# Seven products in place of eight for w2's column chunks, and splits placed two plain blocks ahead, in a float32 decoder layer

## The chip, the core and the metric

The kernel runs on one core of a Trainium2 chip. The core has five engines that run beside each other, each with its own queue in program order, and meet through semaphores: TensorE (PE; PEld is its loading of stationary tiles), VectorE (DVE), ScalarE (ACT), GpSimd (POOL) and SyncE (SP), which here issues most DMAs. The metric is the device time of one execution in microseconds: 2285.92 us before, the median of three runs (2285.74 to 2286.81).

## The reference

One decoder layer on 256 positions of width 2048, in float32: two SwiGLU blocks with a mixer of four branches between them, each behind an RMSNorm and added to the residual x. The change touches the SwiGLUs alone:

```
h = h + 0.5 * swiglu(rms_norm(h, ffn1_norm[l]), ffn1_w1[l], ffn1_w3[l], ffn1_w2[l])
h = h + hybrid_mixer(rms_norm(h, mix_norm[l]), w_in[l], conv_w[l], ...)
h = h + 0.5 * swiglu(rms_norm(h, ffn2_norm[l]), ffn2_w1[l], ffn2_w3[l], ffn2_w2[l])

def swiglu(x, w1, w3, w2):
    return (jax.nn.silu(x @ w1) * (x @ w3)) @ w2
```

w1 and w3 are 2048 x 5632, w2 is 5632 x 2048.

## The kernel before

**Float32 from three products.** The kernel feeds TensorE rounded operands (the type F32R). Each is split into a high part (a cast by ScalarE to the rounded type) and a low part (VectorE: the value minus the high part), and a product a*b is three matmuls: low by high, high by low, high by high. A *step* below is one such matmul of a 128x128 stationary tile with 512 columns.

**Blocks.** The weights stream through in blocks of 256 rows by 512 columns (KB = 2 times 128 rows), 512 KB each. `load` (L254) brings one into a `raw` buffer (six of them), `split` (L268) makes `whi` and `wlo` from it (three buffers each, LA + 1), `multiply` (L292) runs its matmuls. A *plain* block is 2 (rows of 128) x 2 (halves of the 256 positions) x 3 = 12 steps.

**Groups and pairs.** `Group` (L207) is one column chunk: 8 blocks for 2048 rows, two PSUM accumulators. `Pair` (L132) works two chunks with the same stationary side at once, here chunk c of w1 and chunk c of w3: 16 blocks, alternating between the two matrices, four accumulators `acc`. A *quad* is two row blocks by two column chunks, that is two blocks of the list. Six of a pair's eight quads are plain (12 + 12 steps). Quads 0 and 3 (SQ, L27) use a Strassen-like scheme of seven products (`seven`, L162) in place of eight: 21 steps in place of 24. So blocks 0 and 6 of a pair carry no product, and blocks 1 and 7 carry a seven each. For a seven `prepare` (L221) makes sums and differences of the two weight blocks in five steps (step 0: L233 to L235, 1: L237 to L239, 2: L241 to L243, 3: L245 and L246, 4: L248), and `combine` (L384) those of the normalised input, once per SwiGLU and quad; four of the seven products go to `common` (four `wk` banks of PSUM), which `join` (L181) adds up one and two blocks behind the second seven.

**A SwiGLU** (L462) has three parts of 4, 4 and 3 column chunks of h. In each, w1's and w3's chunks come first (chunk 0 as two Groups, the others as Pairs); at the end of a pair `done` and `gated` (L202, L470) add the shares and form h, and `fill` (L413) transposes it through TensorE some blocks later into `hhi` and `hlo`. Then w2 multiplies the part's h into x: four Groups of 8 blocks (6 in part 2), one for each 512 columns of x, and `add` (L484) adds half of each to x from PSUM.

**What sets the order.** Everything is issued by one loop over the blocks (L849). At block i it issues the loads that are due, the split of block i + 2 (LA), the due step of `prepare` (step 5 - j for a seven whose left block is j blocks ahead, LEAD = 5: steps 0 to 4 at five blocks in a row), then block i's matmuls, then the work posted for i (`later`: joins, transposes, combine). Each engine runs its own part strictly in that order; a wait is set where data or a buffer is not there.

Of the kernel before, what the change touches and what calls it, by code (L numbers as in the profile page):

```python
# [14 lines left out]
P = 128  # L15
# [11 lines left out]
SQ = (0, 3)  # L27
LEAD = 5
EPS = 1e-6
# [10 lines left out]
def hybrid_mixer_kernel(  # L40
# [91 lines left out]
    class Pair:  # L132

        n, nk = NQ, NK

        def __init__(self, w1, w3, col0, norm, gated):
            self.norm, self.gated, self.ps = norm, gated, None  # L140
            self.common, self.i0 = None, len(blocks)
            for q in range(NK // KB):
                for w in (w1, w3):
                    ap = w[q * KB * P:(q + 1) * KB * P, col0:col0 + NQ]
                    if q in SQ:
                        early_blocks[len(blocks)] = w is w1
                    blocks.append([self, q * KB, ap.rearrange("(k p) n -> p k n", p=P), None, None])
# [14 lines left out]
        def seven(self, k0, ops7):  # L162
            self.open()
            b11, b21, b22, t1, t2, t3, t4 = ops7
            q = k0 // KB
            s1, s2, s3, s4 = self.norm.sums[q]
            first, last = q == SQ[0], q == SQ[-1]
            a = {(t, k): self.norm.stat(k0 + k, t) for t in range(NT) for k in range(KB)}
# [12 lines left out]
        def join(self, step):  # L181

            c = self.common
            if step == 0:
                c0, u, v, w = (tmp() for _ in range(4))
                self.share = {(0, 0): c0, (0, 1): u, (1, 0): v, (1, 1): w}
                nc.scalar.copy(c0, c[0])
                nc.vector.tensor_add(u, c[1], c0)
                nc.vector.tensor_add(v, c[2], u)
            else:  # L190
                u, v, w = (self.share[i] for i in ((0, 1), (1, 0), (1, 1)))
                nc.vector.tensor_add(u, c[3], u)
                nc.vector.tensor_add(w, c[3], v)

        def plain(self, k0, j, hi, lo):
            for k in range(KB):
                for t in range(NT):
                    last = k0 + k == NK - 1
                    self.product(self.ps[t, j], self.norm.stat(k0 + k, t), (hi[k], lo[k]),
                                 (t, j) == (1, 1) and k0 + k == 2 and 0 in SQ, last)  # L200

        def done(self, _):  # L202
            for i in ((0, 0), (1, 0), (0, 1), (1, 1)):
                nc.vector.tensor_add(self.share[i], self.ps[i], self.share[i])  # L204
            self.gated(self.share)

# [107 lines left out]
    def later(d, f, *a):  # L314
        posts.setdefault(now[0] + d, []).append((f, a))
# [23 lines left out]
    class Norm:  # L339
        def __init__(self, i):  # L340
            self.i = i
            self.ss = sb.tile([P, NT, 4], F32, name=f"ss{i}")
            self.r = sb.tile([P, NT], F32, name=f"rstd{i}")
            self.hi, self.lo = {}, {}
            self.both, self.sums = {}, {}

        def squares(self, c, tiles=range(NT)):
            for t in tiles:
                junk = sb.tile([P, NQ], F32, name="junk")
                nc.scalar.activation(junk, xr[t, c], AF.Square, accum_out=self.ss[:, t, c:c + 1])  # L350
# [32 lines left out]

        def combine(self, q):  # L384

            if not self.sums:
                self.s_hi = ops.tile([P, 2, 4, P], F32R, name="sph", bufs=1)
                self.s_lo = ops.tile([P, 2, 4, P], F32R, name="spl", bufs=1)
            hi, lo = self.both[q]
            v, s = tmp().rearrange("p (k s) -> p k s", k=KB), tmp().rearrange("p (i s) -> p i s", i=4)  # L390
            nc.vector.tensor_add(v, hi.bitcast(F32), lo.bitcast(F32))
# [4 lines left out]
            nc.vector.tensor_sub(s[:, 3], a12, s[:, 1])  # L396
            n = len(self.sums)
            split_to(self.s_hi[:, n], self.s_lo[:, n], s)
            self.sums[q] = [(self.s_hi[:, n, i], self.s_lo[:, n, i]) for i in range(4)]

    class Parts:
# [11 lines left out]
        def fill(self, c, src):  # L413

            hi, lo = self.chunk(c)
            for j in range(2):
# [5 lines left out]
                split_to(hi[:, 2 * j:2 * j + 2], lo[:, 2 * j:2 * j + 2], tp)  # L422

        def stat(self, base):
            def f(k, t):
# [10 lines left out]

    def first_pair(norm, w1, w3, h):

        for j, q in enumerate(SQ):
            posts.setdefault(len(blocks) + 10 + 3 * j, []).append((norm.combine, (q,)))  # L440
        act = {}
# [19 lines left out]

    def swiglu(norm, w1, w3, w2, finish):  # L462
        for part, (c0, c1) in enumerate(((0, 4), (4, 8), (8, 11))):
            h = Parts()
            for c in range(c0, c1):
                if c == 0:
                    first_pair(norm, w1[0], w3[0], h)
                    continue

                def gated(p, i=c - c0, h=h, n=3 if c + 1 == c1 else FILL):  # L470
                    hs = [tmp() for _ in range(NT)]
# [9 lines left out]

                Pair(w1[0], w3[0], c * NQ, norm, gated)
            for c in range(4):
                def add(p, tiles=range(NT), c=c, part=part):  # L484
# [3 lines left out]
                    if part == 2:  # L488
                        finish(c, tiles)

# [16 lines left out]
    def mixer(norm, finish):  # L507
# [239 lines left out]
        qc = to_heads(QC, r8)  # L747
        kc = sb.tile([P, 2, S], F32, name="kc")
        vc = sb.tile([P, NT, P], F32, name="vc")
# [89 lines left out]
    for i in range(LA):  # L839
        norms[0].transposed(0, (i,))  # L840
        split(i)

    turn = sorted(range(5, len(blocks)),
                  key=lambda i: i - 0.5 - LEAD // 2 - (not early_blocks[i]) if i in early_blocks else i)
    at_turn = {}
    for i in turn:
        k = max(0, (i - (not early_blocks[i]) - LEAD - 2) if i in early_blocks else i - 5)
        at_turn.setdefault(k, []).append(i)
# [62 lines left out]
```

## Time and profile before

| | before |
|---|---|
| median of three runs | 2285.92 us |
| the profiled execution | 2286.18 us |
| its span, first to last instruction | 2284.3 us |
| TensorE / VectorE / ScalarE busy | 2257.2 / 1507.4 / 1101.0 us |
| granted TensorE clock, mean | 0.998 |
| matmuls | 10250 |

Matmuls of 512 columns overlap: each is on record for about 0.39 us, but the next starts earlier. So TensorE's pace is read from starts, and a wait shows in brackets behind a row: the idle time before it and who ended it.

### The profile page before, as it was taken

To read this page: it belongs to the slowest core of one execution; us is meant where nothing else is said; L and a number is where in the kernel's file an instruction comes from. 1 tells how busy PE (TensorE), PEld (TensorE's weight loads), DVE (VectorE), ACT (ScalarE), POOL (GpSimd) and SP (SyncE) were. 2 spreads that over 40 slices of the span, in tenths; PEclk is the share of its full clock that TensorE was granted. 3 is DMA by queue.
4 is the path that set the end of the run, shared out by engine and by line. 5 is a ranking of instruction groups with operands and counts; after the bars stand their busy time and mean duration, and the time that the engine had idled before them with its cause. 6 is when DMAs were issued, how large, how long until landed. Compare 5 with 4: busy or idle time off the path is not lost.

```text
span 2284.3 us, 26894 instructions
## 1 busy us (share of the span) xinstructions
PE 2257.2 (99%) x10250; PEld 1854.3 (81%) x10250; DVE 1507.4 (66%) x1765; ACT 1101.0 (48%) x1316; POOL 6.7 (0%) x22
## 2 busy tenths in 40 slices
PE   8999999999999999999999999999999999999998
PEld 6888888888888887778888888888888888888886
DVE  5885587756875566664565555556875678757875
ACT  5554444444545445454565444455544445444543
POOL 0000000000000000000000000000000000000000
PEclk9999999999999999999999999999999999999999
DMA  6565666656655655556655666556665665566564
GB/s 223 185 209 182 194 197 195 192 187 200 187 193 184 192 175 160 170 166 187 182 166 174 193 193 188 185 177 182 203 199 186 195 203 184 184 198 199 184 215 135
DMA packets 222776, 428.56 MB, mean 188 GB/s; under 512 B 13436, under 2 KB 15544, under 8 KB 222648
## 3 DMA queue, kind: packets, MB, share of 16 engines
q1 hardware_dynamic: 222128, 425.78, 59.9%
q8 instruction: 80, 1.31, 0.2%
q10 hardware_dynamic: 520, 1.08, 0.1%
q14 instruction: 48, 0.39, 0.0%
HBM read 424.71 MB, written 2.10 MB: 187 GB/s over the span
## 4 chain that ended last, share of the span: by engine, by line
PE 87%; DVE 8%; ACT 2%; issue 2%; DMA 0%; SPq 0%; POOL 0%; DVEq 0%; POOLq 0%; ACTq 0%
PE acc L307 18%; PE acc L308 18%; PE acc L309 18%; PE acc L159 9%; PE acc L160 9%; PE acc L158 8%; DVE wlo L289 3%; ACT whi L288 1%; DVE tmp L204 1%; PE wk L159 1%; PE wk L160 1%; PE wk L158 1%; PE wk L421 1%; DVE tq L248 1%; DVE at L237 1%
## 5 line engine op out<-in xcount | busy, mean ns | idle before, releaser
L289 DVE TENSOR_TENSOR wlo<-raw,whi 128x1024 fp32r<-128x1024 f32 (+1 forms) x725 | 874.1, 1215 | 643.9 <-ACT whi L288 639.7
L288 ACT CAST whi<-raw 128x1024 fp32r<-128x1024 f32 (+1 forms) x725 | 752.7, 1046 | 821.5 <-PE acc L309 497.0
L307 PE MATMUL acc<-whi,xlo 128*128 128x512 f32 (+1 forms) x992 | 389.0, 392 | 5.5 <-DVE xlo L335 3.7
L308 PE MATMUL acc<-wlo,xhi 128*128 128x512 f32 (+1 forms) x992 | 384.8, 388 | 3.3 <-DVE wlo L289 3.3
L309 PE MATMUL acc<-whi,xhi 128*128 128x512 f32 (+1 forms) x992 | 383.7, 387 | 0.0
L159 PE MATMUL acc<-wlo,xhi 128*128 128x512 f32 x960 | 375.3, 391 | 3.7 <-DVE wlo L289 3.7
L158 PE MATMUL acc<-whi,xlo 128*128 128x512 f32 x960 | 375.0, 391 | 0.0
L160 PE MATMUL acc<-whi,xhi 128*128 128x512 f32 x960 | 373.9, 389 | 0.0
L307 PE MATMUL acc<-whi,hlo 128*128 128x512 f32 x912 | 357.0, 391 | 2.3 <-DVE tmp L204 2.3
L309 PE MATMUL acc<-whi,hhi 128*128 128x512 f32 x912 | 355.2, 389 | 0.0
L308 PE MATMUL acc<-wlo,hhi 128*128 128x512 f32 x912 | 355.2, 389 | 0.0
L307 PEld LDWEIGHTS acc<-whi,xlo 128*128 128x128 f32 x992 | 186.6, 188 | 47.8 <-ACT whi L288 4.6
L308 PEld LDWEIGHTS acc<-wlo,xhi 128*128 128x128 f32 x992 | 186.8, 188 | 41.8 <-DVE wlo L289 5.9
L309 PEld LDWEIGHTS acc<-whi,xhi 128*128 128x128 f32 x992 | 186.8, 188 | 38.1
L159 PEld LDWEIGHTS acc<-wlo,xhi 128*128 128x128 f32 x960 | 180.2, 188 | 45.6 <-DVE wlo L289 9.1
L158 PEld LDWEIGHTS acc<-whi,xlo 128*128 128x128 f32 x960 | 180.3, 188 | 37.1
L160 PEld LDWEIGHTS acc<-whi,xhi 128*128 128x128 f32 x960 | 180.2, 188 | 37.0
L307 PEld LDWEIGHTS acc<-whi,hlo 128*128 128x128 f32 x912 | 171.2, 188 | 39.9 <-issue 5.0
L309 PEld LDWEIGHTS acc<-whi,hhi 128*128 128x128 f32 x912 | 171.2, 188 | 35.9
L308 PEld LDWEIGHTS acc<-wlo,hhi 128*128 128x128 f32 x912 | 171.3, 188 | 35.2 <-DVE wlo L289 0.4
L332 DVE TENSOR_TENSOR hlo<-wk,hhi 128x512 fp32r<-128x512 f32 (+1 forms) x64 | 38.6, 637 | 49.2 <-ACT hhi L331 49.2
L245 ACT CAST tq<-raw 128x1024 fp32r<-128x1024 f32 x40 | 42.2, 1055 | 49.6 <-DVE raw L243 49.6
(205 smaller groups left out, 1739.3 us busy)
## 6 DMA issues: line engine op xcount, KB each, us to landing
raw<-in_ffn_w_dram SPq DMA_DIRECT2D x527, 512.0 KB, 4.1
raw<-in_w_in_dram SPq DMA_DIRECT2D x208, 512.0 KB, 3.6
raw<-in_w_branch_dram SPq DMA_DIRECT2D x32, 512.0 KB, 3.6
raw<-in_w_out_dram SPq DMA_DIRECT2D x32, 512.0 KB, 3.9
x<-in_x_dram SPq DMA_DIRECT2D x8, 256.0 KB, 6.4
raw<-in_w_in_dram SPq DMA_DIRECT2D x8, 256.0 KB, 2.8
out_dram<-x SPq DMA_DIRECT2D x8, 256.0 KB, 2.6
tq<-in_final_norm_dram ACTq DMA_DIRECT2D x2, 512.0 KB, 4.3
```

Source lines behind the costliest of these rows:

```text
L158: nc.tensor.matmul(o, sl, wh, start=start, stop=False)
L159: nc.tensor.matmul(o, sh, wl, start=False, stop=False)
L160: nc.tensor.matmul(o, sh, wh, start=False, stop=stop)
L204: nc.vector.tensor_add(self.share[i], self.ps[i], self.share[i])
L237: nc.vector.tensor_sub(d["bl"], raw1, d["bh"].bitcast(F32))
L245: nc.scalar.copy(d["th1"], raw1)
L288: nc.scalar.copy(h, r)
L289: nc.vector.tensor_sub(l, r, h.bitcast(F32))
L307: nc.tensor.matmul(o, sl, wh, start=(k == 0), stop=False)
L308: nc.tensor.matmul(o, sh, wl, start=False, stop=False)
L309: nc.tensor.matmul(o, sh, wh, start=False, stop=(k == g.nk - 1))
L332: nc.vector.tensor_sub(lo, src, hi.bitcast(F32))
```

## The change

w2 of parts 0 and 1 of each SwiGLU is worked in Pairs too: two pairs of column chunks (0 with 1, 2 with 3) in place of four Groups, each with the two sevens. Part 2 (six row blocks) stays with Groups. `Pair` takes its two matrices, the stationary side, the sums and what to do at the end as arguments. The sums get a class of their own; there is one buffer for them, so they are made for the norm, then for the part's h in the last w1 and w3 pair of the part (blocks 10 and 12), and for the norm again in the second w2 pair (blocks 9 and 11). A w2 pair adds its joined shares to x in the middle (`joined`, in three join steps) and its four accumulators at the end (`rest`).

The loop's plan is new as well. Splits count plain blocks: at a plain block the split of the plain block two further on in the list is issued, so blocks 2 and 3 of a pair are split at blocks 14 and 15 of the one before. Loads come three blocks ahead of the split. The five steps of `prepare` begin 7 blocks ahead of quad 0 and 5 ahead of quad 3, steps 0 and 1 at one block and the rest at the next three: for block 0 at blocks 9 to 12 of the pair before, formerly 11 to 15. The last chunk of h is transposed 10 blocks behind its pair in parts 0 and 1, formerly 3.

```
-LEAD = 5
+LEAD = {0: 7, 3: 5}
 ...
+    class Sums:
+        def make(self, q, both):
+            n = SQ.index(q)
+            if n == 0:
+                self.hi = ops.tile([P, 2, 4, P], F32R, name="sph", bufs=1)
+                self.lo = ops.tile([P, 2, 4, P], F32R, name="spl", bufs=1)
+            hi, lo = both()
+            v = sb.tile([P, KB, S], F32, name="kc", bufs=1)
+            s = sb.tile([P, 4, P], F32, name="junk", bufs=1)
             nc.vector.tensor_add(v, hi.bitcast(F32), lo.bitcast(F32))
 ...
+            split_to(self.hi[:, n], self.lo[:, n], s)
 ...
+        def make_at(self, i, both):
+            for j, q in enumerate(SQ):
+                posts.setdefault(i + 2 * j, []).append((self.make, (q, lambda q=q: both(q))))
 ...
             if last:
-                later(1, self.join, 0)
-                later(2, self.join, 1)
+                for step in range(3 if self.joined else 2):
+                    later(1 + step, self.join, step)
 ...
+                if c + 1 == c1 and part < 2:
+                    h_sums.make_at(len(blocks) + 10, h.both)
+                Pair([w[0][:, c * NQ:(c + 1) * NQ] for w in (w1, w3)], norm.stat, sums, gated)
+            for c in range(0, 4, 2) if part < 2 else ():
+                def joined(i, share, c=c):
+                    y = xr[i[0], c + i[1]]
+                    nc.vector.scalar_tensor_tensor(y, share, 0.5, y, op0=OP.mult, op1=OP.add)
+
+                def rest(p, joined=joined):
+                    for i in ((0, 0), (1, 0), (0, 1), (1, 1)):
+                        joined(i, p[i])
+
+                if c == 2:
+                    sums.make_at(len(blocks) + 9, norm.both.get)
+                Pair([w2[0][c0 * NQ:c1 * NQ, j * NQ:(j + 1) * NQ] for j in (c, c + 1)], h.stat(0),
+                     h_sums, rest, joined)
 ...
+    plain = [i for i in range(len(blocks)) if i not in early_blocks]
+    splits, loads, steps = {}, {}, {}
+    for p in range(LA, len(plain)):
+        n = plain[p - LA]
+        splits[n] = plain[p]
+        if plain[p] >= 5:
+            loads.setdefault(max(0, n - 3), []).append((n, plain[p]))
+    for i, left in early_blocks.items():
+        if left:
+            n = i - LEAD[(blocks[i][1] // KB)]
+            loads.setdefault(n - 2, []).extend([(n, i), (n, i + 1)])
+            for j in range(5):
+                steps.setdefault(n + max(0, j - 1), []).append((i, j))
 ...
-        for j in at_turn.get(i, ()):
+        for _, j in sorted(loads.get(i, ())):
             load(j)
-        split(i + LA)
-        for j in range(1, LEAD + 1):
-            if early_blocks.get(i + j):
-                prepare(i + j, LEAD - j)
+        if i in splits:
+            split(splits[i])
+        for j in steps.get(i, ()):
+            prepare(*j)
```

How this moves VectorE's instructions is seen at two places. The first is the end of an ordinary pair of w1 and w3. Before, the last steps of the next seven's preparation (L246, L248), the closing work (L204, L475, L478), and only then the splits of the next pair's blocks 2 and 3 (L289 x2):

```order
L246 TENSOR_TENSOR tq<-raw,tq 128x1024
L248 TENSOR_TENSOR tq<-raw,tq 128x1024
L204 TENSOR_TENSOR tmp<-acc,tmp 128x512 x4
L475 SCALAR_TENSOR_TENSOR tmp<-tmp,rstd_95 128x512 x2
L478 SCALAR_TENSOR_TENSOR tmp<-tmp,rstd_95 128x512 x2
L289 TENSOR_TENSOR wlo<-raw,whi 128x1024 x2
L235 TENSOR_TENSOR raw<-raw 128x512
L289 TENSOR_TENSOR wlo<-raw,whi 128x1024
```

Now, at the same place (L300 is the split, L215, L501 and L504 the closing work, L246 to L250 steps 0 and 1 of `prepare` for block 7's seven):

```order
L259 TENSOR_TENSOR tq<-raw,tq 128x1024
L300 TENSOR_TENSOR wlo<-raw,whi 128x1024 x3
L215 TENSOR_TENSOR tmp<-acc,tmp 128x512 x4
L501 SCALAR_TENSOR_TENSOR tmp<-tmp,rstd_95 128x512 x2
L504 SCALAR_TENSOR_TENSOR tmp<-tmp,rstd_95 128x512 x2
L246 TENSOR_TENSOR raw<-raw 128x512
L248 TENSOR_TENSOR at<-raw,at 128x1024
L249 TENSOR_TENSOR at<-raw,at 128x512
L250 TENSOR_TENSOR raw<-raw 128x512
L300 TENSOR_TENSOR wlo<-raw,whi 128x1024
```

The splits of blocks 15, 2 and 3 stand ahead of the closing work now, and the preparation of the next seven behind it. The second place is w2 of part 0. Before, its third chunk and the chunk behind it, where VectorE has splits and, per chunk, two additions into x (L486) and nothing else:

```order
L289 TENSOR_TENSOR wlo<-raw,whi 128x1024 x8
L486 SCALAR_TENSOR_TENSOR x_2_82<-acc,x_2_82 128x512
L486 SCALAR_TENSOR_TENSOR x_2_83<-acc,x_2_83 128x512
L289 TENSOR_TENSOR wlo<-raw,whi 128x1024 x4
```

Now, in the second w2 pair, what stands between the preparation of the next pair's block 0 and the split of block 13 (L410 to L343 are half of the sums for the norm, L195 and L196 the second join step, L514 the additions of joined shares into x):

```order
L410 TENSOR_TENSOR kc<-xhi,xlo 128x512
L412 TENSOR_TENSOR junk<-kc 128x128
L413 TENSOR_TENSOR junk<-junk,kc 128x128
L414 TENSOR_TENSOR junk<-kc 128x128
L415 TENSOR_TENSOR junk<-kc,junk 128x128
L343 TENSOR_TENSOR spl<-junk,sph 128x512
L195 TENSOR_TENSOR tmp<-wk,tmp 128x512
L196 TENSOR_TENSOR tmp<-wk,tmp 128x512
L514 SCALAR_TENSOR_TENSOR x_2_83<-tmp,x_2_83 128x512
L300 TENSOR_TENSOR wlo<-raw,whi 128x1024
L253 TENSOR_TENSOR raw<-raw 128x512
L254 TENSOR_TENSOR raw<-raw 128x512
```

Nine instructions stand ahead of the split of block 12 (L300) where before there were splits alone, and in the four rows before these, not shown, steps 0 and 1 of the preparation.

## Rows read from the trace of the kernel before

**Rows 1.** The page, busy us (share of the span) and instructions of each engine.
```profile
PE 2257.2 (99%) x10250; PEld 1854.3 (81%) x10250; DVE 1507.4 (66%) x1765; ACT 1101.0 (48%) x1316; POOL 6.7 (0%) x22
```
**Rows 2.** Timeline of TensorE: start us, us, engine, line, operation, out<-in, count.
```profile
299.73 0.39 PE L158 MATMUL wk<-tq,spl 128*128 128x512 f32 x1
...
312.43 0.39 PE L160 MATMUL acc<-whi,xhi 128*128 128x512 f32 x1
```
**Rows 3.** Waits of TensorE: engine, line, awaited, us in total, times, longest.
```profile
PE acc L159 <- DVE wlo L289: 3.7, 10, 0.4
...
PE acc L307 <- DVE tmp L204: 2.3, 6, 0.4
...
PE wk L159 <- DVE tq L246: 1.1, 1, 1.1
```
**Rows 4.** Timeline of TensorE, one pair of w1 and w3.
```profile
368.79 0.39 PE L158 MATMUL wk<-at,xlo 128*128 128x512 f32 x1
...
374.31 0.50 PE L159 MATMUL acc<-wlo,xhi 128*128 128x512 f32 x1 [0.38 <-DVE wlo L289]
...
389.86 0.39 PE L158 MATMUL acc<-whi,xlo 128*128 128x512 f32 x1
...
400.75 1.03 PE L421 MATMUL wk<-ident,tmp 128*128 128x128 f32 x8
401.54 0.48 PE L158 MATMUL acc<-whi,xlo 128*128 128x512 f32 x1
...
412.53 0.39 PE L158 MATMUL wk<-at,xlo 128*128 128x512 f32 x1
```
**Rows 5.** Timeline of VectorE, the second half of the same pair.
```profile
393.87 1.22 DVE L289 TENSOR_TENSOR wlo<-raw,whi 128x1024 fp32r<-128x1024 f32 x1 [4.79 <-ACT whi L288]
395.01 0.68 DVE L192 TENSOR_TENSOR tmp<-wk,tmp 128x512 f32<-128x512 f32 x1
...
404.58 1.22 DVE L237 TENSOR_TENSOR at<-raw,at 128x1024 fp32r<-128x1024 f32 x1
...
408.18 0.68 DVE L242 TENSOR_TENSOR raw<-raw 128x512 f32<-128x512 f32 x1
...
409.39 1.22 DVE L246 TENSOR_TENSOR tq<-raw,tq 128x1024 fp32r<-128x1024 f32 x1
...
411.74 2.47 DVE L204 TENSOR_TENSOR tmp<-acc,tmp 128x512 f32<-128x512 f32 x4
414.13 1.40 DVE L475 SCALAR_TENSOR_TENSOR tmp<-tmp,rstd 128x512 f32<-128x512 f32 x2
...
416.78 2.35 DVE L289 TENSOR_TENSOR wlo<-raw,whi 128x1024 fp32r<-128x1024 f32 x2
```
**Rows 6.** Timeline of ScalarE, the cast for that split.
```profile
392.78 1.05 ACT L288 CAST whi<-raw 128x1024 fp32r<-128x1024 f32 x1 [5.90 <-PE acc L160]
```
**Rows 7.** Timeline of VectorE, both halves of the second SwiGLU's sums.
```profile
1581.85 0.68 DVE L391 TENSOR_TENSOR tmp<-xhi,xlo 128x512 f32<-128x512 f32 x1
...
1585.24 1.23 DVE L289 TENSOR_TENSOR wlo<-raw,whi 128x1024 fp32r<-128x1024 f32 x1 [0.26 <-ACT whi L288]
...
1593.60 0.68 DVE L391 TENSOR_TENSOR tmp<-xhi,xlo 128x512 f32<-128x512 f32 x1
...
1596.03 0.69 DVE L332 TENSOR_TENSOR spl<-tmp,sph 128x512 fp32r<-128x512 f32 x1 [0.69 <-ACT sph L331]
1596.64 1.22 DVE L246 TENSOR_TENSOR tq<-raw,tq 128x1024 fp32r<-128x1024 f32 x1
```
**Rows 8.** DMA issues, 366 to 420 us: KB each, us to landing.
```profile
raw<-in_ffn_w_dram SPq DMA_DIRECT2D x20, 512.0 KB, 3.7
```
**Rows 9.** Stretches: us, busy (instructions) of each engine, granted clock, DMA.
```profile
43.00:46.00 3.00, 1.22 (x5) 0.44 (x3) 2.51 (x3) 3.00 (x5) 0.00 (x0) 0.99 0.00 0
46.00:49.40 3.40, 3.22 (x8) 2.57 (x9) 3.33 (x6) 0.76 (x1) 0.00 (x0) 0.51 0.61 173
...
1595.00:1600.00 5.00, 3.73 (x16) 2.47 (x15) 4.31 (x7) 4.41 (x5) 0.00 (x0) 1.00 0.31 83
```

More of the change, by code (lines that the diff above doesn't have):

```diff
@@ L137, in hybrid_mixer_kernel, with __init__ @@
         n, nk = NQ, NK
-        def __init__(self, w1, w3, col0, norm, gated):
-            self.norm, self.gated, self.ps = norm, gated, None
+        def __init__(self, w, stat, sums, done, joined=None):
+            self.stat, self.sums, self.finish, self.joined, self.ps = stat, sums, done, joined, None
             self.common, self.i0 = None, len(blocks)
             for q in range(NK // KB):
-                for w in (w1, w3):
-                    ap = w[q * KB * P:(q + 1) * KB * P, col0:col0 + NQ]
+                for j in range(2):
+                    ap = w[j][q * KB * P:(q + 1) * KB * P]
                     if q in SQ:
-                        early_blocks[len(blocks)] = w is w1
+                        early_blocks[len(blocks)] = j == 0
                     blocks.append([self, q * KB, ap.rearrange("(k p) n -> p k n", p=P), None, None])
@@ L165, in seven @@
             q = k0 // KB
-            s1, s2, s3, s4 = self.norm.sums[q]
+            s1, s2, s3, s4 = self.sums.of[q]
             first, last = q == SQ[0], q == SQ[-1]
-            a = {(t, k): self.norm.stat(k0 + k, t) for t in range(NT) for k in range(KB)}
+            a = {(t, k): self.stat(k0 + k, t) for t in range(NT) for k in range(KB)}
             c, o = self.common, self.ps
@@ L189, in join @@
                 nc.vector.tensor_add(v, c[2], u)
-            else:
+                if self.joined:
+                    self.joined((0, 0), c0)
+            elif step == 1:
                 u, v, w = (self.share[i] for i in ((0, 1), (1, 0), (1, 1)))
@@ L193, in join @@
                 nc.vector.tensor_add(w, c[3], v)
+                if self.joined:
+                    self.joined((1, 0), v)
+            else:
+                for i in ((0, 1), (1, 1)):
+                    self.joined(i, self.share[i])
         def plain(self, k0, j, hi, lo):
@@ L198, in plain @@
                     last = k0 + k == NK - 1
-                    self.product(self.ps[t, j], self.norm.stat(k0 + k, t), (hi[k], lo[k]),
+                    self.product(self.ps[t, j], self.stat(k0 + k, t), (hi[k], lo[k]),
                                  (t, j) == (1, 1) and k0 + k == 2 and 0 in SQ, last)
         def done(self, _):
+            if self.joined:
+                self.finish(self.ps)
+                return
             for i in ((0, 0), (1, 0), (0, 1), (1, 1)):
                 nc.vector.tensor_add(self.share[i], self.ps[i], self.share[i])
-            self.gated(self.share)
+            self.finish(self.share)
     class Group:
@@ L382, in stat, with __init__ @@
             return self.hi[k][:, s], self.lo[k][:, s]
[L384 to L390, printed above, removed]
+    class Sums:
+        def __init__(self):
+            self.of = {}
+        def make(self, q, both):
[6 more added lines that the diff above has]
+            s = sb.tile([P, 4, P], F32, name="junk", bufs=1)
             nc.vector.tensor_add(v, hi.bitcast(F32), lo.bitcast(F32))
@@ L435, in hybrid_mixer_kernel, with first_pair @@
     FILL = 2 * SQ[-1] + 6
-    def first_pair(norm, w1, w3, h):
-        for j, q in enumerate(SQ):
-            posts.setdefault(len(blocks) + 10 + 3 * j, []).append((norm.combine, (q,)))
+    def first_pair(norm, w1, w3, h, sums):
+        sums.make_at(len(blocks) + 9, norm.both.get)
         act = {}
@@ L462, in swiglu, with gated @@
     def swiglu(norm, w1, w3, w2, finish):
+        sums = Sums()
         for part, (c0, c1) in enumerate(((0, 4), (4, 8), (8, 11))):
-            h = Parts()
+            h, h_sums = Parts(), Sums()
             for c in range(c0, c1):
                 if c == 0:
-                    first_pair(norm, w1[0], w3[0], h)
+                    first_pair(norm, w1[0], w3[0], h, sums)
                     continue
-                def gated(p, i=c - c0, h=h, n=3 if c + 1 == c1 else FILL):
+                def gated(p, i=c - c0, h=h, n=FILL if c + 1 < c1 else 3 if part == 2 else FILL - 2):
                     hs = [tmp() for _ in range(NT)]
@@ L480, in gated, with add @@
                     later(n, h.fill, i, hs)
-                Pair(w1[0], w3[0], c * NQ, norm, gated)
-            for c in range(4):
-                def add(p, tiles=range(NT), c=c, part=part):
+                if c + 1 == c1 and part < 2:
[9 more added lines that the diff above has]
+                if c == 2:
+                    sums.make_at(len(blocks) + 9, norm.both.get)
+                Pair([w2[0][c0 * NQ:c1 * NQ, j * NQ:(j + 1) * NQ] for j in (c, c + 1)], h.stat(0),
+                     h_sums, rest, joined)
+            for c in range(4) if part == 2 else ():
+                def add(p, tiles=range(NT), c=c):
                     for t in tiles:
```

22 lines of the change are left out of this document (8 added, 14 removed).

## The prediction

> **What bounds the kernel now.** I read the page's busy shares first, then TensorE's pace, then its waits, then the timelines of one pair on three engines. TensorE is busy 99% of the span, VectorE 66%, ScalarE 48% [rows 1]. A busy share hides small losses, so I go by starts: 56 steps of a 128x512 product take 12.70 us [rows 2], 0.2268 us a step, though a record lasts 0.39. Twelve steps make a plain block of 2.72 us, 21 steps a block of seven products of 4.76. The waits that TensorE shows are few and short: ten for the second half of a split at the end of a pair and six for the transposed `h` ahead of a w2 chunk [rows 3].
>
> One pair shows how the engines are coupled [rows 4]. It has 16 blocks, 0 to 15; 0 and 6 carry no product, 1 and 7 the sevens. From its seven at 368.79 to the next pair's at 412.53 are 43.74 us. 186 steps are 42.18, the eight transposes take 0.79 (400.75 to 401.54), so 0.77 is lost: at 374.31 block 2 has waited for its `wlo`, because the 5.04 us of closing work (411.74 to 416.78 for the next pair [rows 5]) stand before that split.
>
> The second half of a pair matters most. Let u be the time since TensorE began block 8 (389.86). The split of block 11 starts at u = 4.01 on VectorE after 4.79 us of idling [rows 5], since ScalarE's cast waits for TensorE to finish block 8 [rows 6]: three `whi` buffers hold 8, 9 and 10. The additions at 395.01, whose products had ended with block 7, stood behind that split all the while. So nothing that is queued behind the split of block 11 can start before u = 5.15, however early its data are.
>
> The Trainium skill says the same in "TensorE: Matmul & The Clock Gate" (the table at its head, and Part 1 on queue depths): VectorE and ScalarE are strict FIFOs, and only TensorE pulls anything ahead. This trace agrees (4.79 us idle with ready work behind). If the engine could reorder, the lags below would vanish and the sum would be that of the first rival.
>
> **The change, part by part.**
>
> *Products.* Eight pairs (two in parts 0 and 1 of each SwiGLU) replace 16 chunks; each has two quads with 21 steps in place of 24: 8 x 6 = 48 steps, 48 x 0.2268 = -10.9 us. All of it is on TensorE's path.
>
> *Splits two plain blocks ahead.* The splits of the next pair's blocks 2 and 3 now stand before the closing work. That work starts when they are through and ends 4.8 us after the pair, the preparation for block 7 (0.61 + 2.46 = 3.07: half of 408.18 to 409.39, and 404.58 to 408.18 less one split of 1.14 [rows 5]) at 7.8, the split of block 4 at 9.0; block 4 needs it at 4.76 + 2 x 2.72 + 0.23 = 10.4. No wait: the ten losses go, 10 x 0.77 = -7.7. Four of the six waits for `h` go too, since that transposing now lies inside a pair (4 x about 0.5 = -2). A new load into a `raw` buffer lands 3.7 us after the buffer is free [rows 8]; the next pair's two loads come after the splits of 12 and 13, at u = 10.6 and 13.0, so they land by 16.7, before their casts. The four loads of the two preparations move up with them on SyncE's queue. I cost the loads at nothing, covered by the two blocks between landing and cast; if the next pair's first load waited for the last preparing step (u = 17.5) it would land at 21.2, the closing work would slip by 2.4 us, and each pair end would lose up to 1.4.
>
> *Preparation of block 0 moved from blocks 11-15 to 9-12.* It then shares blocks 9 to 13 with the joins. In an ordinary pair VectorE's queue from u = 4.01 is: split 1.14 (393.87 to 395.01; its result is there after 1.22), preparation 3.07, join 1.20, split of 12 ending at 10.64; needed at 10.88 + 0.79 + 0.23 = 11.90. Two subtractions 1.21, split of 13 by 12.99 (needed 14.62), 1.14 and `hlo` 1.20, split of 14 by 16.47 (needed 17.34), 1.14, split of 15 by 18.75 (needed 20.06). No wait, with 0.9 to spare. Whatever more is put into this stretch has only that much room, and the change puts in two things.
>
> *Sums.* They are made again four times per SwiGLU beside the first: for `h` in the last pair of w1 and w3, for the norm in the second w2 pair, in parts 0 and 1. Each has two halves. A half takes 3.04 us of VectorE (1593.60 to 1596.64), 0.7 of it a wait for ScalarE's cast, and 3.39 when a split follows, whose cast stands behind that cast (1581.85 to 1585.24) [rows 7]. 16 halves, 49 us or more.
>
> *Additions into x.* Before, eight per part from PSUM; now sixteen per part, half from the joined shares: 0.66 each (414.13 to 416.78 for four [rows 5]; the bounds are 0.60, as for a subtraction, and 0.70, half the 1.40 of the row at 414.13). In a w2 pair one stands before the split of 12 and two before that of 13.
>
> *Last pair before w2.* As the ordinary pair up to the split of 12 (10.56 on VectorE). Then 1.21, half the sums and the cast behind it 3.39, split: ends 16.45, needed 14.71 (block 13): 1.74 late. Block 13 then ends at 18.95. 1.14, 1.20, split of 14 ends 19.93, needed 19.18: 0.75 late; block 14 ends 22.43. 1.14, the other half 3.39, split of 15 ends 25.60, needed 22.66: 2.94 late. Sum 5.4 us.
>
> *First w2 pair.* Here `h`'s last part is transposed after block 9. Split 1.14, preparation 3.07, `hlo` 1.20, join 1.20, addition 0.66: split of 12 ends 12.50, needed 11.90: 0.6 late. 1.21, two additions 1.33, split of 13 about 0.95 late. 14 and 15 in time. 1.5 us.
>
> *Second w2 pair.* No transposes. 5.15; preparation to 8.22; sums to 11.26; join to 12.47; addition to 13.13; split of 12 ends 14.35, needed 11.11: 3.24 late; block 12 ends 16.85. 1.21, two additions 1.33, split of 13 ends 18.03, needed 17.08: 0.95; block 13 ends 20.52. 1.14, sums and cast 3.39, split of 14 ends 23.70, needed 20.75: 2.95. Block 15 in time. 7.1 us.
>
> Together 14.1 us per part, four parts: +56.4. Errors of price add up along such a queue: were the 0.7 of waiting inside each half filled, it would be about 11 per part (+43); were each operation a tenth dearer, about 19 (+76).
>
> *First pair of each SwiGLU.* Sums at blocks 9 and 11 and the preparation at 9 to 12 now fall into the same four blocks; before they were spread to block 15, and TensorE waited 1.1 us once [rows 3]. By the same count (split of 12 late by 1.7, of 14 by 2.55) a pair loses 4.25 now; part of it replaces losses that are there already, so I take +2.5 each, +5. Bounds: -1 (the lag is hidden and the old wait goes) and +8.5.
>
> Sum: -10.9 - 7.7 - 2 + 56.4 + 5 = +40.8. The profiled execution took 2286.18 us (span 2284.3 and 1.9 outside it), 0.3 above the median shown; 2286.2 + 40.8 = 2327.
>
> **Rivals.**
>
> *The lag does not reach TensorE* (faster). If VectorE had the room, because the splits stand further ahead, only the first three terms act, and the first pair costs nothing: 2286.2 - 20.6 = 2266. For it: VectorE is busy only 66% over the span. Against it: 66% is an average over stages; in this stage the queue is gated at u = 4.01 in every pair. It decides from the point where the added work in blocks 9 to 13 falls under 0.9 us; I count 6 to 8.
>
> *Half the lag.* The sums' second halves fall where TensorE is held already, and VectorE saves more than I see in the stretch where it idled: +28 in place of 56: 2299. For it: lags are differences of long sums. Against it: the durations are read from the same operations.
>
> *The clock falls as well.* Between 43 and 46 us TensorE was busy 1.22 of 3.00 us, and then its granted clock was 0.51, the 1.2 GHz level, for 3.4 us: 8 steps in place of 15, 1.6 us [rows 9]. The waits of about 3 us in the last pair and the second w2 pair are as bare. Where such a fall comes before another wait VectorE catches up meanwhile; after the last wait of a pair it is paid: two per part, 8 x 1.6 = +13: 2340. Against it: from 1595 to 1600 TensorE stood for 1.27 of 5.00 us and kept 1.00. The Trainium skill, same page, Part 1 on the clock gate, has the idle array returned to half its clock; the row of 46.00 agrees, and by the rule this rival would be the rule rather than the exception.
>
> *The gains and the lag cancel*: lag of some 20 us, 2286, within the 0.2% (4.6 us) that a measurement of this kernel tells from no change.
>
> **How the numbers follow.** Forecast 2327: 0.48 (its own range 2315 to 2335). Clock as well, 2340: 0.26. Half the lag, 2299: 0.14. Not reaching TensorE, 2266: 0.09. Cancelling: 0.03. Slower 0.88, same 0.03, faster 0.09. The range leaves out the fastest case and the far tail of the clock's: 2290 to 2348.
>
> **What would show it.** TensorE should have 48 matmuls fewer, its ten waits for `wlo` at pair ends should be gone, and its waits for `wlo` should stand at blocks 12 to 15 of the last pair before w2 and of both w2 pairs, the longest about 3 us, behind the sums' lines, 16 times or more. VectorE should show no idle time from the split of block 11 to the end of these pairs but for the sums' casts. An ordinary pair should take 43.0 us. If VectorE idles before the splits of 12 to 15, or a wait for a load stands there, the working is wrong; if the second w2 pair takes under 45 us, so is its size.

## The result, and the profile after

The changed kernel takes 2338.09 us, the median of four runs (2333.01 to 2343.54), against 2286.36 of the kernel before (2285.74 to 2286.81): a ratio of 1.0227, 95% interval 1.0207 to 1.0246. It is slower, as forecast, and the time lies in the range, nearest to the rival in which the clock falls as well (2340). But no run took 2338: two of the four (2333.01, 2333.22) lie inside the likeliest case's own range (2315 to 2335), two (2342.97, 2343.54) above it, and the median falls between them.

The profiled execution is one of the longer ones: 2342.97 us, span 2340.9, mean granted clock 0.989. The page, as in [rows 1]:

```profile
PE 2274.5 (97%) x10202; PEld 1857.5 (79%) x10202; DVE 1640.7 (70%) x2021; ACT 1133.2 (48%) x1372; POOL 6.7 (0%) x22
```

TensorE has 48 matmuls fewer, as worked out. It is on record as busy 17 us longer all the same, since a step behind a wait (0.50 us on record) and a step at half clock (0.63) last longer than an ordinary one (0.39). Its waits, to be held against [rows 3] (engine, line, awaited, us in total, times, longest):

```profile
PE acc L160 <- DVE wlo L300: 24.7, 31, 2.2
PE acc L159 <- ACT whi L299: 16.4, 16, 1.6
...
PE acc L318 <- DVE tmp L215: 0.8, 2, 0.4
```

L159 and L160 are `Pair`'s products. Before, they waited for a split ten times, 3.7 us in all; now 47 times for 41.1. The waits for `h` have gone from six to two.

**An ordinary pair.** TensorE's timeline from one pair's seven to the next two (start us, us, engine, line, operation, out<-in, count), which answers to [rows 4]:

```profile
341.52 0.39 PE L159 MATMUL wk<-at,xlo 128*128 128x512 f32 x1
...
384.59 0.39 PE L159 MATMUL wk<-at,xlo 128*128 128x512 f32 x1
...
389.58 0.39 PE L160 MATMUL acc<-wlo,xhi 128*128 128x512 f32 x1
...
427.64 0.39 PE L159 MATMUL wk<-at,xlo 128*128 128x512 f32 x1
```

A pair takes 43.07 and 43.05 us (43.74 before), and the first low product of block 2, at 389.58, has no bracket: the 0.77 at the pair's end is gone. VectorE shows why, at the same pair end ([rows 5]):

```profile
383.16 1.23 DVE L300 TENSOR_TENSOR wlo<-raw,whi 128x1024 fp32r<-128x1024 f32 x1 [1.40 <-ACT whi L299]
384.30 2.48 DVE L215 TENSOR_TENSOR tmp<-acc,tmp 128x512 f32<-128x512 f32 x4
...
389.34 0.69 DVE L246 TENSOR_TENSOR raw<-raw 128x512 f32<-128x512 f32 x1
```

VectorE is through with the split of block 3 and takes up the closing work at 384.30, before the next pair begins at 384.59; the closing work used to stand ahead of that split.

**The second w2 pair of part 0.** TensorE's rows with a wait in blocks 12 to 14, with the row before each and, twice, the row behind:

```profile
279.69 0.39 PE L161 MATMUL acc<-whi,hhi 128*128 128x512 f32 x1
280.65 0.50 PE L159 MATMUL acc<-whi,hlo 128*128 128x512 f32 x1 [0.57 <-ACT whi L299]
283.36 0.50 PE L160 MATMUL acc<-wlo,hhi 128*128 128x512 f32 x1 [2.21 <-DVE wlo L300]
...
285.99 0.39 PE L159 MATMUL acc<-whi,hlo 128*128 128x512 f32 x1
286.91 0.50 PE L160 MATMUL acc<-wlo,hhi 128*128 128x512 f32 x1 [0.53 <-DVE wlo L300]
287.25 0.39 PE L161 MATMUL acc<-whi,hhi 128*128 128x512 f32 x1
...
289.31 0.39 PE L161 MATMUL acc<-whi,hhi 128*128 128x512 f32 x1
291.30 0.49 PE L159 MATMUL acc<-whi,hlo 128*128 128x512 f32 x1 [1.60 <-ACT whi L299]
292.56 0.80 PE L160 MATMUL acc<-wlo,hhi 128*128 128x512 f32 x1 [0.76 <-DVE wlo L300]
293.15 0.63 PE L161 MATMUL acc<-whi,hhi 128*128 128x512 f32 x1
```

What a wait costs is read from start to start, less the 0.23 of a step: block 12 loses 0.96 + 2.71 - 2 x 0.23 = 3.2 us, block 13 0.7, block 14 2.8 (from 289.31 to 292.56, two waits). The whole pair takes 50.72 us, from its seven to the next:

```profile
248.64 0.39 PE L159 MATMUL wk<-at,hlo 128*128 128x512 f32 x1
...
299.36 0.39 PE L159 MATMUL wk<-at,xlo 128*128 128x512 f32 x1
```

The last pair of w1 and w3 in part 0 and its first w2 pair, TensorE's waits alone (blocks 13, 13, 14, 15, 15; then 12 and 13; from start to start each costs some 0.2 more than its bracket):

```profile
191.10 0.50 PE L159 MATMUL acc<-whi,xlo 128*128 128x512 f32 x1 [0.48 <-ACT whi L299]
192.36 0.50 PE L160 MATMUL acc<-wlo,xhi 128*128 128x512 f32 x1 [0.76 <-DVE wlo L300]
...
195.83 0.50 PE L160 MATMUL acc<-wlo,xhi 128*128 128x512 f32 x1 [0.45 <-DVE wlo L300]
...
200.22 0.50 PE L159 MATMUL acc<-whi,xlo 128*128 128x512 f32 x1 [1.58 <-ACT whi L299]
201.48 0.50 PE L160 MATMUL acc<-wlo,xhi 128*128 128x512 f32 x1 [0.76 <-DVE wlo L300]
...
237.02 0.50 PE L160 MATMUL acc<-wlo,hhi 128*128 128x512 f32 x1 [0.32 <-DVE wlo L300]
...
240.57 0.50 PE L160 MATMUL acc<-wlo,hhi 128*128 128x512 f32 x1 [0.53 <-DVE wlo L300]
```

In all, 1.7 + 0.6 + 2.8 = 5.1 us in the one and 0.5 + 0.7 = 1.2 in the other.

VectorE in the second w2 pair (L246 to L259 are the preparation, L410 to L343 half the sums, L195 the join, L514 additions into x):

```profile
273.04 1.23 DVE L300 TENSOR_TENSOR wlo<-raw,whi 128x1024 fp32r<-128x1024 f32 x1 [4.26 <-ACT whi L299]
...
277.25 0.68 DVE L410 TENSOR_TENSOR kc<-xhi,xlo 128x512 f32<-128x512 f32 x1
...
279.68 0.69 DVE L343 TENSOR_TENSOR spl<-junk,sph 128x512 fp32r<-128x512 f32 x1 [0.69 <-ACT sph L342]
280.29 0.68 DVE L195 TENSOR_TENSOR tmp<-wk,tmp 128x512 f32<-128x512 f32 x1
...
281.49 0.68 DVE L514 SCALAR_TENSOR_TENSOR x<-tmp,x 128x512 f32<-128x512 f32 x1
282.09 1.22 DVE L300 TENSOR_TENSOR wlo<-raw,whi 128x1024 fp32r<-128x1024 f32 x1
...
291.28 1.23 DVE L300 TENSOR_TENSOR wlo<-raw,whi 128x1024 fp32r<-128x1024 f32 x1 [0.25 <-ACT whi L299]
```

It idles 4.26 us ahead of the split of block 11, and then works from 273.04 to 291.28 with no gap but 0.69 and 0.68 us for the sums' casts and 0.25 for the split's cast behind the second. ScalarE has its part in the waits: its cast for block 12 stands behind the sums' cast at 279.03, so TensorE waits first for `whi`, then for `wlo`.

**The clock.** Windows of the stretch behind block 14's wait (us; busy and instructions of PE, PEld, DVE, ACT, POOL; granted clock; DMA share; GB/s), and of a stretch that holds as long a wait in the last pair before w2, with the one behind it:

```profile
288.00:292.20 4.20, 2.19 (x9) 1.25 (x7) 3.19 (x7) 2.52 (x4) 0.00 (x0) 1.00 0.75 244
292.20:295.60 3.40, 3.04 (x7) 2.46 (x8) 3.40 (x4) 0.94 (x1) 0.00 (x0) 0.50 0.56 161
...
198.00:201.50 3.50, 1.16 (x5) 0.40 (x3) 2.56 (x6) 2.90 (x4) 0.00 (x0) 1.00 0.71 224
201.50:206.00 4.50, 4.50 (x20) 3.69 (x21) 4.50 (x6) 2.24 (x4) 0.00 (x0) 1.00 0.65 227
```

Seven matmuls run in 3.4 us where full clock has fifteen. Ahead of its last 10 us this execution has twelve stretches at half clock, one of them 6.8 us long; the kernel before has one (46.00 in [rows 9]). Four stand in the first 70 us or behind the first pair of the second SwiGLU (8.9, 46.5, 63.5 and 1623.4 us), eight behind long waits of the last pairs and the second w2 pairs. There are twelve such long waits (block 15 of a last pair, blocks 12 and 14 of a second w2 pair), so the clock fell behind eight of twelve. By TensorE's starts, 89 steps begin about 0.2 us late with no wait before them, 7 in the kernel before: 17.4 us of late steps for 1.4. Behind the waits at 198 to 201.5 the clock stayed at 1.00.

### The profile page after: what moved, and what is told of

Read it like the earlier page. It is cut to its first block, busy times and chain, and to the rows that moved or that the text cites. A ratio compares the mean times of both kernels' runs of the same rounds, so it can differ in the third digit from the quotient of the medians.

```text
span 2340.9 us, 27074 instructions
## 1 busy us (share of the span) xinstructions
PE 2274.5 (97%) x10202; PEld 1857.5 (79%) x10202; DVE 1640.7 (70%) x2021; ACT 1133.2 (48%) x1372; POOL 6.7 (0%) x22
## 4 chain that ended last, share of the span: by engine, by line
PE 87%; DVE 8%; ACT 2%; issue 2%; POOL 0%; ACTq 0%; POOLq 0%; DVEq 0%
PE acc L318 13%; PE acc L319 13%; PE acc L320 13%; PE acc L160 13%; PE acc L161 13%; PE acc L159 12%; DVE wlo L300 3%; PE wk L159 2%; PE wk L160 2%; PE wk L161 2%; ACT whi L299 2%; DVE at L248 1%; PE wk L443 1%; DVE hlo L343 0%; DVE raw L246 0%
## 5 line engine op out<-in xcount | busy, mean ns | idle before, releaser
L300 DVE TENSOR_TENSOR wlo<-raw,whi 128x1024 fp32r<-128x1024 f32 (+1 forms) x693 | 837.5, 1215 | 564.3 <-ACT whi L299 562.7
L299 ACT CAST whi<-raw 128x1024 fp32r<-128x1024 f32 (+1 forms) x693 | 719.1, 1045 | 704.3 <-PE acc L161 336.1
L159 PE MATMUL acc<-whi,xlo 128*128 128x512 f32 x960 | 377.5, 393 | 8.3 <-ACT whi L299 8.3
L160 PE MATMUL acc<-wlo,xhi 128*128 128x512 f32 x960 | 376.7, 392 | 7.9 <-DVE wlo L300 7.9
L160 PEld LDWEIGHTS acc<-wlo,xhi 128*128 128x128 f32 x960 | 181.4, 189 | 49.0 <-DVE wlo L300 12.1
L159 PEld LDWEIGHTS acc<-whi,xlo 128*128 128x128 f32 x960 | 181.1, 189 | 48.6 <-ACT whi L299 11.7
L160 PE MATMUL acc<-wlo,hhi 128*128 128x512 f32 x384 | 155.8, 406 | 16.9 <-DVE wlo L300 16.9
L159 PE MATMUL acc<-whi,hlo 128*128 128x512 f32 x384 | 153.8, 401 | 8.1 <-ACT whi L299 8.1
L318 PE MATMUL acc<-whi,hlo 128*128 128x512 f32 x400 | 157.0, 393 | 0.8 <-DVE tmp L215 0.8
L319 PE MATMUL acc<-wlo,hhi 128*128 128x512 f32 x400 | 155.9, 390 | 0.0
L320 PE MATMUL acc<-whi,hhi 128*128 128x512 f32 x400 | 155.7, 389 | 0.0
L161 PE MATMUL acc<-whi,hhi 128*128 128x512 f32 x384 | 152.8, 398 | 0.0
L160 PEld LDWEIGHTS acc<-wlo,hhi 128*128 128x128 f32 x384 | 74.3, 193 | 39.0 <-DVE wlo L300 24.0
L252 ACT CAST tq<-raw 128x1024 fp32r<-128x1024 f32 x56 | 58.9, 1052 | 92.8 <-DVE raw L250 92.8
```

What stands on the lines that cost most here:

```text
L159: nc.tensor.matmul(o, sl, wh, start=start, stop=False)
L160: nc.tensor.matmul(o, sh, wl, start=False, stop=False)
L161: nc.tensor.matmul(o, sh, wh, start=False, stop=stop)
L252: nc.scalar.copy(d["th0"], raw3)
L299: nc.scalar.copy(h, r)
L300: nc.vector.tensor_sub(l, r, h.bitcast(F32))
```

## The experiments

All ran beside the kernel before, whose median stayed between 2286.0 and 2286.4.

**The change once more**, unaltered, to see what its spread is.

> The change once more, unaltered, on the chip of the next three. Both theories: 2333 to 2344 us, as in its four runs so far, which fall into two groups 10 us apart.

Measured 2339.14 us (2333.15 to 2343.75), ratio 1.0229 [1.0207, 1.0252]. The eight runs of this program fall into two groups: 2333.0, 2333.2, 2333.2, 2334.9 and 2343.0, 2343.4, 2343.5, 2343.8. Its profile is of the shorter kind (span 2332.8, clock 0.993). Near 565 us both profiles show the same two waits (1.60, then 0.77 and 0.76), but behind them the clock differs. First the longer execution, then the shorter:

```profile
565.30:572.10 6.80, 6.12 (x14) 4.79 (x15) 4.03 (x4) 2.28 (x4) 0.00 (x0) 0.50 0.74 240
```
 
and in the shorter one, where 28 matmuls ran in place of 14:

```profile
565.30:572.10 6.80, 6.39 (x28) 5.30 (x29) 6.24 (x8) 3.01 (x4) 0.00 (x0) 1.00 0.76 240
```

The clock means differ by 0.004; at half clock that is 2 x 0.004 x 2341 = 19 us of stretches, which cost half of it, 9.4 us. By starts, the late steps are 17.4 us and 8.6. The groups lie 10 apart, and the clock means of all eight runs go with them: 0.993 in the shorter four, 0.989 or 0.990 in the longer. In the shorter profile the clock fell behind four of the twelve long waits, not eight.

**Ten unread matmuls before block 15 of each last pair and blocks 12 and 14 of each second w2 pair**, so that TensorE works where it stood; nothing else changes.

```
+        if isinstance(g, Pair) and i - g.i0 in g.warm:
+            o = ps.tile([P, NQ], F32, name="wk")
 ...
+            for _ in range(10):
+                nc.tensor.matmul(o, a, b, start=True, stop=True)
```

> Ten matmuls of 512 columns whose result nobody reads are put ahead of block 15 of the last pair before w2 and ahead of blocks 12 and 14 of the second w2 pair: 2.3 us of TensorE work inside waits of 2.8 to 3.2 us, twelve places in all. Theory 1 with the clock (the lag of VectorE's queue makes the waits, and bare waits of this length let TensorE's clock fall, which is paid on top): the waits end when they did, the falls at these places go, mean granted clock 0.995 or more, 2324 to 2330 us. Rival (the clock is not part of it): 2338 or more, since what the fillers overrun is added.

Measured 2329.59 us (2328.19 to 2330.43), ratio 1.0187 [1.017, 1.0204], clock 0.997. TensorE at block 14 of the second w2 pair (L922 are the added matmuls):

```profile
289.91 0.39 PE L162 MATMUL acc<-whi,hhi 128*128 128x512 f32 x1
290.14 2.43 PE L922 MATMUL wk<-xhi 128*128 128x512 f32 x10
292.40 0.39 PE L160 MATMUL acc<-whi,hlo 128*128 128x512 f32 x1
293.17 0.50 PE L161 MATMUL acc<-wlo,hhi 128*128 128x512 f32 x1 [0.38 <-DVE wlo L301]
```

The lag is what it was: 2.49 + 0.77 - 2 x 0.23 = 2.8 us. But the clock no longer falls behind it:

```profile
292.20:295.60 3.40, 3.02 (x14) 2.18 (x13) 3.40 (x4) 1.55 (x2) 0.00 (x0) 1.00 0.32 92
```

So 120 more matmuls made the kernel 8.5 to 9.6 us faster than the two medians of the change, and the two groups of runs are gone; in this profile the clock fell behind none of the twelve waits. That part of the loss is clock, not lag, and the rival that gave the clock no part (2338 or more) falls.

**No remade sums**: w2's sevens take the norm's sums, so their part of the computation is left out.

```
-                    h_sums.make_at(len(blocks) + 10, h.both)
 ...
-                    sums.make_at(len(blocks) + 9, norm.both.get)
```

> The sums are not made again: w2's sevens take the norm's sums in place of those of h (this part of the computation is left out). Eight pairs of halves fewer on VectorE. Theory 1 (the lag is the work between the splits of blocks 11 and 15, the sums above all): the last pair before w2 loses nothing, both w2 pairs about 1.2 each through the additions, 2286.2 - 20.6 + 9.4 + 5 = 2280, within 2274 to 2288. Rival A (the earlier preparation or the additions make the lag): above 2310.

Measured 2283.7 us (2283.24 to 2284.86), ratio 0.999 [0.9981, 0.9999]; TensorE's waits for `Pair`'s `wlo` fall from 24.7 us to 5.4 and those for its `whi` are no longer in the list:

```profile
PE acc L160 <- DVE wlo L300: 5.4, 12, 0.5
```

With the sums 54 us go; twelve short waits are left. Whether it is their amount or their place, this run doesn't tell.

**The same sums at block 8**, both halves, ahead of the split of block 11, where VectorE idles.

```
-                    h_sums.make_at(len(blocks) + 10, h.both)
+                    h_sums.make_at(len(blocks) + 8, h.both, 0)
 ...
-                    sums.make_at(len(blocks) + 9, norm.both.get)
+                    sums.make_at(len(blocks) + 8, norm.both.get, 0)
```

> All sums are made, as often as in the change, but both halves stand behind block 8, ahead of the split of block 11, where VectorE idles 4.4 us for the buffer of block 8. Theory 1 (it is the place in the queue): the last pair before w2 loses under 0.5, the first w2 pair 1.5 as before, the second about 2.9 in place of 7.1: about 9 us less per part, 2288 to 2300. Rival B (it is VectorE's added work, wherever it stands): 2330 or more.

Measured 2298.38 us (2298.21 to 2300.62), ratio 1.0055 [1.004, 1.007]. The same instructions, 40 us less (late steps at half clock included): it is the place, and the rival of the amount (2330 or more) falls. In the second w2 pair of part 0 one wait is left of five, since both halves now stand ahead of one split:

```profile
278.33 0.50 PE L160 MATMUL acc<-wlo,hhi 128*128 128x512 f32 x1 [2.43 <-DVE wlo L300]
```

**The new plan alone**, with w2 in four Groups and no remade sums.

```
-            for c in range(0, 4, 2) if part < 2 else ():
+            for c in ():
 ...
-            for c in range(4) if part == 2 else ():
+            for c in range(4):
```

> The change's new order of splits, loads and preparations alone: w2 goes as four Groups in all parts, as before, and the h sums and the remade norm sums are gone. Theory (the lag comes from the sums that stand among the preparations): no pair has them but the first of each SwiGLU, so the ten losses at pair ends go (2286.2 - 7.7) and the first pairs keep their lag (+5): 2284, range 2278 to 2291, no wait over 1 us outside the first pairs. Rival (the preparations for block 0, moved from blocks 11 to 15 up to 9 to 12, delay the splits by themselves): at least 2300, with waits for wlo in the second half of ordinary pairs.

Measured 2286.15 us (2285.31 to 2288.34), ratio 0.9999 [0.999, 1.0008]. The ten waits for `wlo` in `Pair` are not in its list, so I take the -7.7 as earned; what eats it is then 2286.15 - (2286.2 - 7.7) = +7.7, where +5 was counted for the first pairs. In part it is the clock: its profiled execution (2288.34, the longest of its eleven) has 5.5 us of late steps, 1.4 before, all but one of them in the first 70 us or behind the first pair of the second SwiGLU. The rival (2300 or more) falls. Taken alone, half of the change does nothing.

**The pairs of w2 alone**, with the sums as in the change but the plan of before (preparation for block 0 at blocks 11 to 15).

```
-LEAD = {0: 7, 3: 5}
+LEAD = 5
 ...
+        split(i + LA)
+        for j in range(1, LEAD + 1):
+            if early_blocks.get(i + j):
+                prepare(i + j, LEAD - j)
```

> The pairs of w2 with their sums as in the change, but with the order of splits, loads and preparations of the kernel before: the preparation for block 0 goes to blocks 11 to 15, one step at each, not to 9 to 12. Theory (lag from nine instructions that stand between two splits with steps 0 to 2 of the preparation among them): the sums at blocks 9 and 11 now stand where only splits are, so the split of block 12 is in time and the lags of the second w2 pairs shrink to those at blocks 13 to 15; the losses at pair ends stay (+7.7 and eight more pairs x 0.77 = 6): 2295 to 2318. Rival (the lag belongs to the extra pairs and their sums, wherever the preparation stands): 2333 to 2350.

Measured 2304.33 us (2304.1 to 2305.38), ratio 1.0081 [1.0067, 1.0095]. All its waits in the second w2 pair of part 0:

```profile
280.23 0.50 PE L159 MATMUL acc<-whi,hlo 128*128 128x512 f32 x1 [0.69 <-ACT whi L299]
281.49 0.51 PE L160 MATMUL acc<-wlo,hhi 128*128 128x512 f32 x1 [0.76 <-DVE wlo L300]
285.09 0.50 PE L160 MATMUL acc<-wlo,hhi 128*128 128x512 f32 x1 [0.60 <-DVE wlo L300]
```

Block 12 no longer waits and the pair loses 2.7 us in place of 6.7. The two halves of the change are worth 0 and +18 apart, and +52 together: they meet in the second half of a pair, and part of the 52 is the clock, which stays at 0.997 here. The rival that the place of the preparation doesn't matter (2333 or more) falls.

**The additions into x only at the end of a w2 pair**, all else as in the change.

```
-                     h_sums, rest, joined)
+                     h_sums, rest)
```

> The change with one thing undone: the joined shares of a w2 pair are added to x at its end, with the accumulators, not in its middle; the sums stay where the change has them. Theory (each instruction that stands ahead of a split in the second half of a pair delays it by its length): the 1.2 us lost in each first w2 pair go, and in each second w2 pair the addition of 0.68 us ahead of the split of block 12 no longer counts and two later ones neither: 4 x (1.2 + 0.7 to 2.0) = 8 to 13, less a stretch or two at half clock: 2322 to 2331. Rival (the additions lie in the shadow of the sums): 2335 to 2342.

Measured 2322.28 us (2319.05 to 2323.94), ratio 1.0155 [1.014, 1.0171]. The first w2 pair of part 0 has no wait left, and in the second the one for `wlo` at block 12 is 1.61 us in place of 2.21. In its profile, 21 us shorter than the change's, TensorE's waits by starts are 14 us less and its late steps 4.7 (12.7 for 17.4). I had counted 8 to 13 for the waits. By starts, the first w2 pairs lose 4.7 us less in all and the second ones 10.3: no part waits at block 13 any more, and in three of them block 14 loses 0.8 in place of up to 2.8. The rival (2335 or more) falls.

**All sums moved**, and the additions at the end: the `h` sums at block 8, the norm's first half at block 8 of the second w2 pair and its second half at block 3 of the next pair, the first pair's at blocks 13 and 15.

```
-        sums.make_at(len(blocks) + 9, norm.both.get)
+        sums.make_at(len(blocks) + 13, norm.both.get)
 ...
+                    h_sums.make_at(len(blocks) + 8, h.both, 0)
 ...
+                    sums.make_at(len(blocks) + 8, norm.both.get, 11)
```

> All remade sums moved to where VectorE idles, with the same amount of work: both halves of the h sums at block 8 of the last w1 and w3 pair, the norm's first half at block 8 of the second w2 pair and its second half at block 3 of the next pair, the first pair's at blocks 13 and 15; and the shares of a w2 pair are added to x at its end only. Theory (place in the queue, not amount): of the forecast's sum the -10.9 of the products, the -7.7 of the pair ends and the -2 for h stay, and the lags go: 2286.2 - 20.6 = 2266, range 2262 to 2276, granted clock at least 0.996. Rival (the extra VectorE work costs by its amount, 1640 us busy in place of 1507): not under 2286.

Measured 2270.48 us (2269.66 to 2271.14), ratio 0.9932 [0.992, 0.9944], clock 0.998: faster than both kernels, 0.7% faster than the one before, and the rival of the amount falls. TensorE's waits on `Pair`'s lines:

```profile
PE wk L160 <- DVE tq L259: 2.4, 4, 0.6
...
PE acc L160 <- DVE wlo L300: 1.3, 4, 0.3
```

VectorE is busy 1634.7 us here, 6 less than in the change and 127 more than before. In the second w2 pair the first half of the sums now lies ahead of the split of block 11:

```profile
253.13 1.23 DVE L300 TENSOR_TENSOR wlo<-raw,whi 128x1024 fp32r<-128x1024 f32 x1 [1.25 <-ACT whi L299]
254.27 0.69 DVE L410 TENSOR_TENSOR kc<-xhi,xlo 128x512 f32<-128x512 f32 x1
...
260.66 1.23 DVE L300 TENSOR_TENSOR wlo<-raw,whi 128x1024 fp32r<-128x1024 f32 x1 [1.18 <-ACT whi L299]
```

Of the 4.26 us of idling 1.18 are left ahead of that split, and the splits behind it no longer hold TensorE.

**Both second halves at block 4 of the next pair**, behind the last step of the preparation.

```
-                    h_sums.make_at(len(blocks) + 8, h.both, 0)
+                    h_sums.make_at(len(blocks) + 8, h.both, 12)
 ...
-                    sums.make_at(len(blocks) + 8, norm.both.get, 11)
+                    sums.make_at(len(blocks) + 8, norm.both.get, 12)
```

> The version with all sums moved, with the second half of each remade sum moved once more: the first half of the h sums and of the norm sums stays at block 8, the second half stands at block 4 of the next pair, behind the last step of the preparation for block 7 and ahead of two splits that have slack (in the version before it, the h sums stood both at block 8 and the norm's second half at block 3, ahead of that step; there TensorE still lost 0.6 and 0.2 us behind block 8 of each last pair and 0.75 us at the seven of the next first pair). Theory (only the place in the queue counts): those 1.5 us a part go, 4 x 1.5 = 6: 2264.5, range 2260 to 2268. Rival (what is left does not hang on the place): 2269 to 2272.

Measured 2275.59 us (2274.75 to 2276.16), ratio 0.9953 [0.9941, 0.9966]: a miss, slower than the version it was to improve. The waits it was to remove are gone, and the seven at block 7 waits for the sums themselves:

```profile
210.61 0.50 PE L159 MATMUL wk<-tq,spl 128*128 128x512 f32 x1 [1.39 <-DVE spl L343]
```

I had counted the slack of the splits and not that of the sums: block 6 carries no product, so the seven follows block 5 at once. Neither expectation fits: the place decides, but 1.3 to 1.5 us a pair are lost at this one. The version before it stays the best.

## Why the prediction was right, and where it was not

*Products and pair ends* (-10.9, -7.7, -2): right. 48 matmuls, ordinary pairs of 43.07 and 43.05 for a forecast 43.0, two waits for `h` left of six. *Loads at nothing*: right; a load now takes 4.8 us to land (3.7 in [rows 8]), and TensorE and VectorE show no wait for one (ScalarE two, of 0.4 and 0.3 us; before, four of 1.8 in all).

*The lag per part*: right in mechanism, a little high. By starts, part 0 loses 1.7, 0.6 and 2.8 us at blocks 13, 14 and 15 of the last pair (forecast 1.74, 0.75, 2.94), 0.5 and 0.7 at 12 and 13 of the first w2 pair (0.6, 0.95), and 3.2, 0.7 and 2.8 in the second (3.24, 0.95, 2.95): 12.9 for 14.1, and by four parts +51.7 for +56.4. Over the four parts of this execution the same reading gives 12.9, 12.9, 11.7 and 13.0, 50.5 in all: in the third a fall of the clock stands behind block 12 (1845.3 us), block 13 then has no wait and block 14 loses 2.2 in place of 2.8, so VectorE does catch up there, as the prediction had it. Part of the difference are the additions: from 281.49 to 282.09 one takes 0.60, the lower bound that I gave, not 0.66. (One small slip: by its own terms the last pair's split of block 13 ends at 16.38 and is needed at 14.62, so 1.76 late, not 1.74.) The rivals of no lag and of half the lag fell with these rows, and the two runs with moved sums showed that the term hangs on the place: the same work costs +52 us or next to nothing.

*First pair of each SwiGLU*: +5 was too little. TensorE loses 3.9 us in the first (52 to 62.5 us) and 4.2 in the second, 8.1, near the 4.25 each that I had counted. What I took off for losses that were there already was too much: before, the first has none in that place and the second 1.6 (1596.42 to 1599.04 us), so +6.5, and a stretch at half clock follows each. The plan run alone measures +7.7 for all of it.

*The clock*: this step failed. The forecast chose, between its two cases, the one without falls, and put the term at nothing. The step was "after the last wait of a pair it is paid: two per part, 8 x 1.6 = +13", held at 0.26. With the sizes measured, the rest of the sum is 2286.2 - 20.6 + 51.7 + 6.5 = 2323.8: without the falls the forecast was sound. The late steps add 17.4 - 1.4 = 16.0 in the profiled execution (2339.8 of 2343.0), 7.2 in the shorter one (2331.0 of 2334.9), and 3.1 with the waits filled (4.5 us of late steps, all but one of them in the first 70 us, where nothing was filled; 2326.9 of 2330.3). In all three, 3.2 to 3.9 us are left over. Starts place most of it: the step right behind a wait begins 0.11 us late at full clock (287.25 behind 286.91) and mostly 0.36 at half (293.15 behind 292.56), and no term above holds that. Over all waits it comes to 3.6, 3.3 and 2.1 us more than before.

The size of the clock term was right: behind the eight long waits the late steps are 11.8 us in the longer execution, and the forecast had 13 for eight falls. Their number was not fixed: eight, four, and none with the waits filled. The falls in the first 70 us and behind the first pair of the second SwiGLU (5.5 us of late steps, 1.2 before) stood in no case of the forecast. So the median's closeness to 2340 is in part luck: it lies between two groups of runs that the prediction did not foresee. Filling shows that the loss hangs on TensorE standing idle; why some waits are followed by a fall and others not, no run here shows.

The row that I held against the fall, 1595 to 1600 at 1.00 [rows 9], was no counterweight: the same program, behind the same waits, has the clock at 0.50 in one execution and at 1.00 in another. A single row of that kind shows that a fall can be missed, not that it is unlikely. The Trainium skill, "TensorE: Matmul & The Clock Gate", Part 1 on the clock gate, returns an idle array to half its clock; the trace agrees at 292.2, for one, and behind 198 to 201.5 it does not. The prediction read from it that such falls would be the rule; they came behind eight of the twelve long waits in one execution and four in another, and against that the chance of 0.26 was too little.

## What to carry to other kernels

Where an engine works strictly in order, added work is priced by what stands behind it in the queue, not by its length: count from the point where the queue is gated, and put the new work ahead of that point, in the idle time. Two edits that each cost nothing or little alone can meet in the same few blocks. When the sum finds bare waits of 2 to 3 us on TensorE, add the half clock behind them as a cost of its own, in the likeliest case and not in a rival (here some 1.5 us a fall, behind a third to two thirds of the waits), and widen the range by what the falls can differ from one execution to the next.

## What the runs showed of the hardware beyond that

The same waits, equal to 0.01 us, are followed by a granted clock of 0.50 or 1.00 from one execution to the next, which makes two groups of times 10 us apart on one program; with the waits filled the spread is 2.2 us. And a program with 120 matmuls more ran 9 us faster.
